# Moving GpSimd's tensor_tensor work to VectorE in a two-layer diffusion step, with more load buffers at the start and 370 GB/s for transfers in the list schedule

## The chip, the cores and the metric

The kernel runs on one core of one Trainium2 chip. The metric is the device time of one execution in microseconds (us), the median of several runs. Engines are named as in the profile: PE is TensorE (matmuls; PEld its weight loads), DVE is VectorE, ACT is ScalarE, POOL is GpSimd, SP is SyncE, which issues every DMA of this kernel.

## The reference

One inference step of a diffusion backbone, two layers deep, in float32. There are 512 latent tokens and 128 context tokens, handled together as five tiles of 128 tokens. Per layer:

```
mod = silu(cond) @ w_mod + b_mod                 # 6 vectors of 1024, one set for latents, one for context
h = rmsnorm(x) * (1 + sc1) + sh1
z = h @ w_in                                     # queries, keys, values of three mixers, and the gates
mix A: windowed attention with a sink; mix B: latent attention; mix C: full attention with rotary
m = sum over mixers of sigmoid(gate) * (o @ w_o) ;  x = x + g1 * rmsnorm(m @ w_out)
h = rmsnorm(x) * (1 + sc2) + sh2
x = x + g2 * rmsnorm(square(relu(h @ w_mlp1)) @ w_mlp2)      # 1024 -> 4096 -> 1024
```

The outputs are the two token sets and, for the context tokens, each layer's keys and values.

## The kernel before

**Arithmetic.** Nearly every matmul is done with float32 operands split in two: a high part (ACT, a copy to the reduced type) and a low part (DVE, source minus high part), and three products high*high, high*low, low*high (`mm3`). So each weight tile costs one ACT and one DVE instruction beside its matmuls. The split of a loaded weight unit is `wh`/`wl` in the profile.

**Stages of a layer.** First the modulated norm; then the projections and heads of mixer B (`b_proj`, `b_rope`, `b_heads`); then mixers A and C (`gqa_proj`, `gqa_qproj`, `gqa_group`), called the A/C stage below; then the gated merge (`merge`), the output projection (`wout`), the first MLP matrix (the up stage: `mlp1_first`, `sums`, `mlp1_pair`) and the second (the down stage: `mlp2_block`, `kblock`). The modulation vectors of later stages (`mod_gen`) and the gates (`gate_gen`) are side streams that are fed in between. In the first layer the A/C stage lies at about 300 to 550 us and the up stage at 780 to 970; in the second at 1450 to 1700 and 1940 to 2120.

**The up stage.** Output columns are taken in 14 pairs of 128-column tiles per layer. `mlp1_pair` forms a seven-product scheme: it loads a 128 x 2048 block `wq`, forms four sums `s1..s4` of its quarters (the profile's `s`, from lines with `tt = ...`), splits seven operands, and multiplies each by a split block of the activations or of the activation sums `t0..t3` that `sums` makes once per layer out of `hfull`.

**The modulation stream.** `mod_gen` multiplies each 128x512 piece of `w_mod` by a per-partition scalar and accumulates it, for two conditionings: `macc` 0 with one DVE instruction, `macc` 1 with a scaling on ACT and an addition on POOL.

**What POOL does.** Its tensor_tensor work is: the second `macc`, the four sums of each pair, the last addition of the rotary embedding (`ra`), the merge's addition (`m`), the residual addition of the first two token tiles (`xr`), the context's softmax normalisation (`pt<-pt,den`) and 128x1 or 128x4 powers (`rs`, `hrs`). It also does tensor_scalar work with one tensor input: the softmax normalisation of the latents (`pt<-pt,rc`) and the first norm's scaling (`xn`).

**The start.** `first_norm` loads the five token tiles `x` (three buffers) and eight 128 x 2048 blocks `mw` of `w_mod` (four buffers), multiplies the latter by the conditioning on PE (64 matmuls `lps<-mw,scT`), transposes the normed tokens on PE (`nps`) and modulates them.

**What sets the order.** The program is recorded, not issued: `Recorder.record` gives each operation a cost (`cost`), `one` simulates the engines with these costs and takes at each moment the ready operation of lowest rank, `latest` walks back from the end and gives every operation its latest start, which is the rank in the next of eight passes; PE keeps its program order as rank. The plan with the earliest end is emitted, so each engine's instruction order is fixed by it. In the plan a POOL tensor_tensor with over four elements per partition (`both`) runs 1.2 times as long, and a DVE operation without a PSUM operand that meets one is lengthened by up to 0.62 of the overlap. A DMA is planned on one shared network at 300 GB/s (line 470 in `one`), after 1.6 us and with 0.7 us behind it. SP takes its transfers in planned order. All instructions have line 528 in the profile, where the plan is emitted, so rows are told apart by tile names.

Of the kernel before, what the change touches and what calls it, by code (L numbers as in the profile page):

```python
# [11 lines left out]
F32 = mybir.dt.float32  # L12
F32R = mybir.dt.float32r
AF = mybir.ActivationFunctionType
# [3 lines left out]
P = 128  # L18
D = 1024
# [148 lines left out]
class Recorder:  # L168
# [192 lines left out]
    def latest(self, everything, end):  # L361

        for o in everything:
            o.late = end
        before, gave = {}, {}
        last = None
        for o in self.done:
            if o.eng == "tensor":
                before[o], last = last, o
        for p, t in self.given:  # L370
            gave.setdefault(t, []).append(p)
        for o in reversed(self.done):
            for p, data in o.preds.items():
                t = o.late
                if data:
                    t -= p.end - p.start
                    if o.eng is not None and p.eng != o.eng:
                        t -= self.LAT
                p.late = min(p.late, t)
            for p in gave.get(o, ()):  # L380
                p.late = min(p.late, o.late)
            p = before.get(o)
            if p is not None:
                p.late = min(p.late, o.late - p.busy)

    def one(self, everything, look):
# [49 lines left out]
        while True:  # L436
            best = None
            for e in engines:
                if now[e]:
                    t = free[e]  # L440
                elif later[e]:
                    t = max(free[e], later[e][0][0])
                else:
                    continue
                if best is None or t < best[0]:
                    best = (t, e)
            if best is None:
                break
            t, e = best
            ready, soon = now[e], later[e]  # L450
            while soon and soon[0][0] <= t:
                _, c, o = heapq.heappop(soon)
                heapq.heappush(ready, (o.rank, c, o))
            if look and soon and e in ("vector", "scalar", "gpsimd"):

                come = [r for r, c, u in heapq.nsmallest(6, soon) if r < t + ready[0][2].busy and u.rank < ready[0][0] - self.URGENT]
                if come:
                    fit = [q for q in ready if t + q[2].busy <= come[0] + 0.03]
                    if not fit:
                        free[e] = come[0]  # L460
                        continue
                    q = min(fit)
                    ready.remove(q)
                    heapq.heapify(ready)
                    heapq.heappush(ready, (-1e9, q[1], q[2]))
            o = heapq.heappop(ready)[2]
            o.start = t
            busy, wait = o.time
            if o.dma:
                net = max(net, t + 1.6) + wait / 300e3  # L470
                wait = net + 0.7 - t
            elif e == "vector" and o.sb and pool_end > t:
                more = 0.62 * min(pool_end - t, busy / 0.38)
                busy, wait = busy + more, wait + more
            elif o.both:
                busy, wait = 1.2 * busy, 1.2 * wait
                pool_end = t + busy
            elif e == "tensor":
                if t - free[e] > 2.6:
                    half = t + (6.8 if t - free[e] > 4 else 3.4)  # L480
                if t < half:
                    busy, wait = 2 * busy, wait + busy
            free[e] = t + busy
            o.busy, o.end = busy, t + wait
            order.append(o)
            self.done.append(o)
            release([o])
# [44 lines left out]
class Step:  # L532
# [182 lines left out]
    def mod_gen(self, mp, l, vecs, own=0):  # L715
# [3 lines left out]
        for v in vecs:  # L719
            for hf in range(2):  # L720
                c0 = v * D + hf * 512
                acc = [mp.tile([P, 512], F32, name=f"macc{s}", tag=f"macc{s}", bufs=1) for s in range(2)]
                for u in range(4):
# [6 lines left out]
                    for j in range(2):  # L730
                        k = 2 * u + j
                        s0, s1 = self.scT[:, 0, k:k + 1], self.scT[:, 1, k:k + 1]
                        if k == 0:
                            nc.vector.tensor_scalar(acc[0], rv[:, j, :], s0, None, ALU.mult)
                            nc.scalar.activation(acc[1], rv[:, j, :], AF.Copy, scale=s1)
                        else:
                            nc.vector.scalar_tensor_tensor(out=acc[0], in0=rv[:, j, :], scalar=s0, in1=acc[0],
                                                           op0=ALU.mult, op1=ALU.add)
                            nc.scalar.activation(rv[:, j, :], rv[:, j, :], AF.Copy, scale=s1)
                            nc.gpsimd.tensor_tensor(acc[1], acc[1], rv[:, j, :], ALU.add)  # L740
                    yield
                isg = v in (2, 5)
                if isg:
# [79 lines left out]
    def first_norm(self, pool, xin):  # L823

        nc, I = self.nc, self.I
        self.cond()
        xs = [pool.tile([P, D], F32, name="x0", tag="x0", bufs=3) for t in range(NT)]
        for t in range(NT):
            nc.sync.dma_start(xs[t], xin[t])
        hf = pool.tile([P, KC, T], F32, name="hf0")  # L830
# [12 lines left out]
        for n in range(2):  # L843
            if n == 1:
                self.first = self.proj_units(I["w_in"][0], 768 + 384, 288, 3)
            for v in (1, 0):
                ps = self.lin_ps()
                for kh in range(2):
                    raw = pool.tile([P, 4, 512], F32, name="mw", tag="mw", bufs=4)
                    nc.sync.dma_start(raw, self.wsrc(w, 4 * kh, 4, v * D + n * 512, 512))  # L850
                    for i in range(4):
                        k = 4 * kh + i
# [287 lines left out]
    def prompt_group(self, pool, qT, kT, kv, sink):  # L1140
# [22 lines left out]
            nc.scalar.activation(es, es, AF.Exp)  # L1163
            nc.vector.tensor_tensor(den, den, es, ALU.add)
        nc.vector.reciprocal(den, den)
        nc.gpsimd.tensor_tensor(p3, p3, den.unsqueeze(2).to_broadcast([P, 4, P]), ALU.mult)
        yield
        self.ppt = pt

# [27 lines left out]
    def kv_evac(self, pool, l, mixer, kT, V):  # L1197
# [3 lines left out]
        def evac(t, ps):  # L1201
# [6 lines left out]
            def turn():  # L1208
                if norm:
                    norm()  # L1210
                if t < 4:
                    cs = (self.cosA, self.sinA) if isA else (self.cosK, self.sinK)
                    res["k"] = self.rope(pool, k, 2, cs[0][:, t], cs[1][:, t], 16, nc.gpsimd)
                    self.put_v(V, t, v)
                else:
                    if not isA:
# [17 lines left out]
    def q_evac(self, pool, mixer, qT):  # L1234
# [3 lines left out]
        def evac(t, ps):  # L1238
# [5 lines left out]
            def turn():  # L1244
                if norm:
                    norm()
                if t < 4:
                    cs = (self.cosA, self.sinA) if isA else (self.cosQ, self.sinQ)
                    res["q"] = self.rope(pool, q, 4, cs[0][:, t], cs[1][:, t], 16, nc.gpsimd)
                elif isA:  # L1250
                    res["q"] = q
                else:
# [160 lines left out]
    def b_rope(self, keep, pool, l):  # L1413
# [5 lines left out]
        for t in range(NT):  # L1419
# [4 lines left out]
                         wl[:, k].rearrange("p h d -> p (h d)"), k == 0, k == 2)  # L1424
            pv = ps[:, :256].rearrange("p (h d) -> p h d", h=8)
            if t < 4:
                r = self.rope(pool, pv, 8, self.cosB[:, t], self.sinB[:, t], 8, nc.gpsimd)
                nc.scalar.activation(self.qr[:, t], r, AF.Copy)
            else:
                nc.scalar.activation(self.qr[:, t], pv, AF.Copy)  # L1430
# [161 lines left out]
    def merge(self, pool, l, mh, ml):  # L1592
# [12 lines left out]
        for n2 in range(4):  # L1605
# [5 lines left out]
            for i, b in enumerate((1, 0, 2)):  # L1611
                for e in range(2):
# [12 lines left out]
                        out=dst.rearrange("p (a n) -> p a n", a=2), in0=th.rearrange("p (a n) -> p a n", a=2), scalar=1.0,  # L1625
                        in1=ps[:, :, :NH], op0=ALU.add, op1=ALU.mult)
                    if i:
                        nc.gpsimd.tensor_tensor(m, m, th, ALU.add)
                    yield
            for e in range(2):  # L1630
                n, m = 2 * n2 + e, ms[e]
# [51 lines left out]
    def post(self, pool, l, w, src, f, t, xsrc, out):  # L1683
# [7 lines left out]
        r = self.rstd(src, D, jk, 2 if last or src is not f else 1)  # L1691
        for c in (slice(0, 512), slice(512, D)) if last else (slice(0, D),):
            nc.vector.scalar_tensor_tensor(out=f[:, c], in0=src[:, c], scalar=r, in1=self.gg[:, s, c], op0=ALU.mult, op1=ALU.mult)
            (nc.vector if t >= 2 else nc.gpsimd).tensor_tensor(x[:, c], x[:, c], f[:, c], ALU.add)
            nc.sync.dma_start(out[:, c], x[:, c])
        return x

# [67 lines left out]
    def mlp1_pair(self, pool, l, n, t, halfs, keep=None):  # L1765
# [7 lines left out]
        sa = pool.tile([P, 2, 4, P], F32, name="s12", tag="s12", bufs=2)  # L1773
        sb = pool.tile([P, 2, 4, P], F32, name="s34", tag="s34", bufs=2)
        s1, s2, s3, s4 = sa[:, 0], sa[:, 1], sb[:, 0], sb[:, 1]
        tt = nc.gpsimd.tensor_tensor
        tt(s1, a21, a22, ALU.add)
        tt(s2, s1, a11, ALU.subtract)
        tt(s3, a11, a21, ALU.subtract)
# [376 lines left out]
```

## Time and profile before

| quantity | value |
| --- | --- |
| median of 3 runs | 2357.48 us (2355.71 to 2359.46) |
| profiled execution | 2356.36 us, span 2354.6 us, mean granted clock 0.995 |
| PE busy | 2286.6 us (97%) |
| DVE busy | 1700.6 us (72%) |
| ACT busy | 1289.2 us (55%) |
| POOL busy | 763.2 us (32%) |
| DMA | 317 MB, mean 135 GB/s |

The span is the profiled execution from its first to its last instruction; what lies around it is 1.8 us. Busy is the time in which an engine had an instruction running. Ends of matmuls are modelled and overlap with the next one, so a busy PE can still have lost some time; where that matters, matmuls are counted per stretch instead.

### The profile page before, as it was taken

What the parts mean: (1) busy time and instruction counts of PE and PEld (TensorE: products, weight loads), DVE (VectorE), ACT (ScalarE), POOL (GpSimd) and SP (SyncE); (2) the same over time, 40 slices, a digit from 0 to 9 for tenths busy, and PEclk for the clock granted to TensorE, in tenths of its full rate; (3) what the DMA queues carried; (4) which work ended last, traced back from release to release, by engine and by line L of the source; (5) the groups of instructions that cost most, each with busy time, mean ns of one, the idle gap of its engine ahead of it and who ended that gap; (6) DMA issues with size and microseconds to landing.
All of it is one profiled execution on the core that took longest, in us unless ns stands there. A gap on an engine that the chain in (4) does not pass through costs nothing. (4 is left out here: it accounts for less than half of the span.)

```text
span 2354.6 us, 39546 instructions
## 1 busy us (share of the span) xinstructions
PE 2286.6 (97%) x14303; PEld 2089.6 (89%) x14303; DVE 1700.6 (72%) x3351; ACT 1289.2 (55%) x3000; POOL 763.2 (32%) x671
## 2 busy tenths in 40 slices
PE   8999999999999999999999999999999999999998
PEld 3988999989998999888889889899999889998886
DVE  3778488897675998867477866998846669884444
ACT  4577466676435565744265765767743356664222
POOL 1322044562132475223033212455412315650001
PEclk9999999999999999999999999999999999999999
DMA  7431244343663454664244222434346544446332
GB/s 252 112 91 50 86 121 129 104 107 96 218 208 113 149 170 146 224 209 150 80 134 113 65 82 75 127 105 125 109 152 187 177 135 150 165 139 215 117 120 81
DMA packets 252451, 317.10 MB, mean 135 GB/s; under 512 B 37328, under 2 KB 169696, under 8 KB 251744
## 3 DMA queue, kind: packets, MB, share of 16 engines
q1 hardware_dynamic: 252256, 314.58, 42.9%
q8 instruction: 113, 1.85, 0.3%
q14 instruction: 82, 0.67, 0.1%
HBM read 251.84 MB, written 57.44 MB: 131 GB/s over the span
## 5 line engine op out<-in xcount | busy, mean ns | idle before, releaser
L528 DVE TENSOR_TENSOR wl<-wr,wh 128x256 fp32r<-128x256 f32 (+5 forms) x772 | 370.5, 527 | 145.0 <-ACT wh L528 143.6
L528 ACT ACTIVATE wh<-wr 128x256 fp32r<-128x256 f32 (+5 forms) x772 | 276.2, 421 | 257.5 <-PE lps L528 140.0
L528 POOL TENSOR_SCALAR pt<-pt,rc 128x640 f32<-128x640 f32 (+1 forms) x192 | 167.4, 879 | 315.3 <-DVE rc L528 261.2
L528 PE MATMUL lps<-wh,ah 128*128 128x512 f32 x640 | 252.8, 395 | 0.0
L528 PE MATMUL lps<-wh,al 128*128 128x512 f32 x640 | 252.4, 394 | 0.0
L528 PE MATMUL lps<-wl,ah 128*128 128x512 f32 x640 | 251.9, 394 | 0.0
L528 POOL TENSOR_TENSOR rs<-ss,mhalf 128x1 f32<-128x1 f32 x60 | 37.1, 619 | 497.5 <-DVE ss L528 496.6
L528 DVE TENSOR_TENSOR pl<-tps,ph 128x512 fp32r<-128x512 f32 (+2 forms) x240 | 147.8, 631 | 30.3 <-ACT ph L528 27.6
L528 ACT ACTIVATE pt<-sps,nm 128x640 f32<-128x640 f32 (+2 forms) x192 | 141.7, 741 | 50.9 <-DVE nm L528 48.6
L528 PE MATMUL sps<-h2h,wl 128*128 128x320 f32 (+2 forms) x464 | 145.0, 313 | 9.8 <-DVE wl L528 9.8
L528 ACT ACTIVATE ph<-tps 128x512 fp32r<-128x512 f32 (+2 forms) x240 | 130.4, 555 | 33.0 <-PE tps L528 29.9
L528 PE MATMUL sps<-h2h,wh 128*128 128x320 f32 (+2 forms) x464 | 145.9, 314 | 0.0
L528 PE MATMUL tps<-ident,pt 128*128 128x128 f32 x896 | 140.5, 275 | 5.2 <-POOL pt L528 1.9
L528 PEld LDWEIGHTS lps<-wl,ah 128*128 128x128 f32 x640 | 120.1, 188 | 28.5 <-issue 0.2
L528 PEld LDWEIGHTS lps<-wh,ah 128*128 128x128 f32 x640 | 120.1, 188 | 28.0 <-issue 0.5
L528 PE MATMUL sps<-h2l,wh 128*128 128x320 f32 (+2 forms) x464 | 144.6, 312 | 0.0
L528 PEld LDWEIGHTS lps<-wh,al 128*128 128x128 f32 x640 | 120.1, 188 | 27.5
L528 POOL TENSOR_TENSOR macc<-macc,wr 128x512 f32<-128x512 f32 x84 | 118.3, 1409 | 57.2 <-ACT wr L528 44.4
L528 POOL TENSOR_TENSOR s<-wq 128x512 f32<-128x512 f32 x56 | 89.8, 1604 | 142.4 <-DMA wq<-in_w_mlp 116.9
L528 POOL TENSOR_TENSOR macc<-macc,mr 128x512 f32<-128x512 f32 x56 | 87.7, 1566 | 140.5 <-ACT mr L528 92.9
L528 DVE TENSOR_TENSOR wl<-s,wh 128x512 fp32r<-128x512 f32 x112 | 123.3, 1114 | 3.4 <-ACT wh L528 2.2
L528 PE MATMUL gps<-hh,wh 128*128 128x320 f32 x384 | 120.1, 313 | 2.2 <-ACT th L528 1.7
(335 smaller groups left out, 7371.4 us busy)
## 6 DMA issues: line engine op xcount, KB each, us to landing
wr<-in_w_in SPq DMA_DIRECT2D x72, 512.0 KB, 3.8
wr<-in_w_mlp SPq DMA_DIRECT2D x72, 512.0 KB, 4.0
wq<-in_w_mlp SPq DMA_DIRECT2D x56, 512.0 KB, 4.1
wr<-in_w_mod SPq DMA_DIRECT2D x48, 512.0 KB, 3.8
ar<-a SPq DMA_DIRECT2D x56, 320.0 KB, 4.5
mr<-in_w_mod SPq DMA_DIRECT2D x32, 512.0 KB, 4.6
th<-th SPq DMA_DIRECT2D x96, 160.0 KB, 1.9
tg<-th SPq DMA_DIRECT2D x48, 320.0 KB, 3.1
```

What stands on the lines that cost most here:

```text
L528: getattr(getattr(self.nc, o.eng), o.name)(*args, **kw)
```

## The change

All POOL tensor_tensor instructions over whole tiles become DVE instructions. In `mod_gen` the pair "scale on ACT, add on POOL" becomes one DVE scalar_tensor_tensor. POOL keeps the powers and the tensor_scalar work. The first norm gets five buffers for `x` and eight for `mw`. The plan counts transfers with 370 GB/s, and in the backward pass a transfer counts its own 2.3 us plus bytes/370e3 in place of the time between its planned issue and landing.

```
             for p, data in o.preds.items():
                 t = o.late
                 if data:
-                    t -= p.end - p.start
+                    t -= 2.3 + p.wait / 370e3 if p.dma else p.end - p.start
...
-                net = max(net, t + 1.6) + wait / 300e3
+                net = max(net, t + 1.6) + wait / 370e3
...   mod_gen
-                            nc.scalar.activation(rv[:, j, :], rv[:, j, :], AF.Copy, scale=s1)
-                            nc.gpsimd.tensor_tensor(acc[1], acc[1], rv[:, j, :], ALU.add)
+                            nc.vector.scalar_tensor_tensor(out=acc[1], in0=rv[:, j, :], scalar=s1, in1=acc[1],
+                                                           op0=ALU.mult, op1=ALU.add)
...   first_norm
-        xs = [pool.tile([P, D], F32, name="x0", tag="x0", bufs=3) for t in range(NT)]
+        xs = [pool.tile([P, D], F32, name="x0", tag="x0", bufs=5) for t in range(NT)]
-                    raw = pool.tile([P, 4, 512], F32, name="mw", tag="mw", bufs=4)
+                    raw = pool.tile([P, 4, 512], F32, name="mw", tag="mw", bufs=8)
...   prompt_group
-        nc.gpsimd.tensor_tensor(p3, p3, den.unsqueeze(2).to_broadcast([P, 4, P]), ALU.mult)
+        nc.vector.tensor_tensor(p3, p3, den.unsqueeze(2).to_broadcast([P, 4, P]), ALU.mult)
...   kv_evac, q_evac, b_rope: rope(..., nc.gpsimd) becomes rope(..., nc.vector)
...   merge
-                        nc.gpsimd.tensor_tensor(m, m, th, ALU.add)
+                        nc.vector.tensor_tensor(m, m, th, ALU.add)
...   post
-            (nc.vector if t >= 2 else nc.gpsimd).tensor_tensor(x[:, c], x[:, c], f[:, c], ALU.add)
+            nc.vector.tensor_tensor(x[:, c], x[:, c], f[:, c], ALU.add)
...   mlp1_pair
-        tt = nc.gpsimd.tensor_tensor
+        tt = nc.vector.tensor_tensor
```

## Rows read from the trace of the kernel before

**Rows 1.** The page's engines: busy us (share of the span), instructions.
```profile
PE 2286.6 (97%) x14303; PEld 2089.6 (89%) x14303; DVE 1700.6 (72%) x3351; ACT 1289.2 (55%) x3000; POOL 763.2 (32%) x671
```

**Rows 2.** Waits of PE, whole span: us in total, times, longest us.
```profile
PE sps L528 <- DVE wl L528: 9.8, 2, 5.1
...
PE nps L528 <- POOL xn L528: 2.8, 1, 2.8
```

**Rows 3.** Stretches where the up stages begin: busy us (instructions), PEclk, DMA share, GB/s.
```profile
785.00:790.00 5.00, 1.11 (x5) 1.11 (x6) 5.00 (x4) 2.81 (x7) 4.92 (x4) 0.91 0.00 0
...
1940.00:1945.00 5.00, 0.33 (x1) 0.33 (x2) 5.00 (x4) 2.03 (x5) 4.92 (x4) 0.78 0.00 0
1945.00:1950.00 5.00, 5.00 (x21) 5.00 (x21) 5.00 (x4) 3.41 (x9) 4.14 (x3) 0.54 0.16 52
```

**Rows 4.** Timeline of DVE, second up stage: start us, us, what.
```profile
1932.78 0.82 DVE L528 TENSOR_TENSOR t1l<-hfull,t1h 128x640 fp32r<-128x640 f32 x1
...
1935.72 3.75 DVE L528 TENSOR_TENSOR t0l<-hfull,t0h 128x640 fp32r<-128x640 f32 x2
1939.39 1.75 DVE L528 TENSOR_TENSOR wl<-wq,wh 128x512 fp32r<-128x512 f32 x1
...
1950.35 0.68 DVE L528 TENSOR_TENSOR wl<-wq,wh 128x512 fp32r<-128x512 f32 x1
```

**Rows 5.** Timeline of POOL in the same stretch.
```profile
1935.59 1.38 POOL L528 TENSOR_TENSOR s<-wq 128x512 f32<-128x512 f32 x1 [17.02 <-DMA wq<-in_w_mlp]
```

**Rows 6.** Timeline of PE in the same stretch.
```profile
1944.67 0.64 PE L528 MATMUL sps<-h2h,wl 128*128 128x320 f32 x1 [5.12 <-DVE wl L528]
```

**Rows 7.** Groups of instructions, whole span: count | busy us, mean ns.
```profile
L528 POOL TENSOR_TENSOR macc<-macc,wr 128x512 f32<-128x512 f32 x84 | 118.3, 1409 | 57.2 <-ACT wr L528 44.4 <-issue 6.9 <-DVE rc L528 2.2
L528 POOL TENSOR_TENSOR s<-wq 128x512 f32<-128x512 f32 x56 | 89.8, 1604 | 142.4 <-DMA wq<-in_w_mlp 116.9 <-DVE u L528 8.8 <-DVE wl L528 8.3
L528 POOL TENSOR_TENSOR m<-m,tg 128x640 f32<-128x640 f32 x32 | 55.1, 1723 | 186.5 <-DMA tg<-th 87.6 <-DVE tg L528 79.3 <-issue 10.9
L528 DVE TENSOR_TENSOR wl<-s,wh 128x512 fp32r<-128x512 f32 x112 | 123.3, 1114 | 3.4 <-ACT wh L528 2.2
```

**Rows 8.** Stretches inside the first A/C stage and the first up stage.
```profile
300.00:550.00 250.00, 240.79 (x1751) 228.97 (x1751) 224.46 (x506) 163.86 (x418) 123.37 (x117) 1.00 0.41 119
800.00:950.00 150.00, 150.00 (x1017) 149.04 (x1016) 133.85 (x190) 92.50 (x158) 94.94 (x59) 1.00 0.50 165
```

**Rows 9.** Groups of instructions between 300 and 550 us.
```profile
L528 DVE TENSOR_TENSOR wl<-wr,wh 128x256 fp32r<-128x256 f32 x80 | 43.3, 585 | 0.9 <-ACT wh L528 0.8
L528 DVE SCALAR_TENSOR_TENSOR macc<-wr,scT,macc 128x512 f32<-128x512 f32 x35 | 30.8, 881 | 0.4
...
L528 POOL TENSOR_TENSOR ra<-ra,rb 128x256 f32<-128x256 f32 x12 | 11.1, 928 | 16.7 <-DVE rb L528 11.1 <-DVE hss L528 4.2 <-DVE ra L528 1.4
```

**Rows 10.** Timeline of DVE where POOL has nothing to do.
```profile
1912.39 1.41 DVE L528 SCALAR_TENSOR_TENSOR f<-fps,rs,gg 128x512 f32<-128x512 f32 x2 [0.66 <-POOL rs L528]
...
1914.92 1.42 DVE L528 TENSOR_TENSOR wl<-wr,wh 128x256 fp32r<-128x256 f32 x4
```

**Rows 11.** Timelines of DVE and of POOL in the A/C stage, one moment.
```profile
481.46 1.52 DVE L528 TENSOR_TENSOR pz<-pz,hrs 128x256 f32<-128x256 f32 x1
...
481.26 1.44 POOL L528 TENSOR_TENSOR macc<-macc,wr 128x512 f32<-128x512 f32 x1
```

**Rows 12.** Stretches of the start.
```profile
28.00:32.00 4.00, 1.17 (x8) 1.10 (x8) 0.89 (x5) 1.95 (x5) 1.77 (x2) 0.91 1.06 389
32.00:36.00 4.00, 4.00 (x16) 1.22 (x15) 0.96 (x5) 1.29 (x3) 0.00 (x0) 0.66 1.06 393
```

**Rows 13.** Timelines of SP and PE at the start.
```profile
20.20 0.38 SPq L528 DMA_DIRECT2D x<-in_x_prompt  x1
...
30.90 1.62 PE L528 MATMUL nps<-ident,xn 128*128 128x128 f32 x8 [2.83 <-POOL xn L528]
```

**Rows 14.** DMA issues on the page: count, KB each, median us to landing.
```profile
wr<-in_w_in SPq DMA_DIRECT2D x72, 512.0 KB, 3.8
```

More of the change, by code (lines that the diff above doesn't have):

```diff
@@ L1212, in turn @@
                     cs = (self.cosA, self.sinA) if isA else (self.cosK, self.sinK)
-                    res["k"] = self.rope(pool, k, 2, cs[0][:, t], cs[1][:, t], 16, nc.gpsimd)
+                    res["k"] = self.rope(pool, k, 2, cs[0][:, t], cs[1][:, t], 16, nc.vector)
                     self.put_v(V, t, v)
@@ L1248, in turn @@
                     cs = (self.cosA, self.sinA) if isA else (self.cosQ, self.sinQ)
-                    res["q"] = self.rope(pool, q, 4, cs[0][:, t], cs[1][:, t], 16, nc.gpsimd)
+                    res["q"] = self.rope(pool, q, 4, cs[0][:, t], cs[1][:, t], 16, nc.vector)
                 elif isA:
@@ L1426, in b_rope @@
             if t < 4:
-                r = self.rope(pool, pv, 8, self.cosB[:, t], self.sinB[:, t], 8, nc.gpsimd)
+                r = self.rope(pool, pv, 8, self.cosB[:, t], self.sinB[:, t], 8, nc.vector)
                 nc.scalar.activation(self.qr[:, t], r, AF.Copy)
```

## The prediction

> **What bounds the kernel now.** The page's engine line comes first: PE is busy 97% of the span, DVE 72%, POOL 32% [rows 1]. So a change that touches no matmul can win only what PE loses. A busy PE hides part of that, since ends of matmuls are modelled; the matmuls of a stretch, counted, show it. Inside an up stage PE issues 1017 matmuls in 150 us, one per 0.1475 us, without a gap [rows 8]; there nothing can be won. The list of what PE waited for comes second. Its largest line is a wait for `wl`, 9.8 us in two pieces [rows 2]: both lie where the up stages begin, one per layer. The third view is a table of stretches there: PE has 5 matmuls in one 5 us stretch of the first layer, and 1 and then 21 in two such stretches of the second, where 34 would fit, and the granted clock of these falls to 0.78 and 0.54 [rows 3], so in part to the lower of the two levels. The fourth view is the start, with a wait of 2.8 us for the last token tile [rows 2], again with a lower clock behind it, 0.66 [rows 12]. In the first A/C stage PE is idle for 250 - 240.8 = 9.2 us, in small pieces, beside a DVE that is busy 224.5 of 250 us [rows 8].
>
> **The beginning of the up stage.** The stall of PE is a chain on DVE. Two `t0l` take 3.75 us, a split `wl` 1.75 us; the neighbouring `t1l` of the same shape took 0.82 us and a later split of the same shape 0.68 us [rows 4]. What differs is POOL: from 1935.59 us on it forms the sums `s` [rows 5]. So each of these DVE instructions loses about 1 us. The stall ends with a `wl` at 1944.67 us after 5.12 us [rows 6], and the matmuls behind it come 0.24 us apart (21 in 5 us [rows 3]) instead of 0.1475, until the clock is back.
>
> After the change POOL does nothing here, and DVE does the four sums itself. I lay DVE's work for the first pair out from 1935.72 us, when PE still has matmuls up to 1939.5 us (1944.67 less 5.12 [rows 6]). The distance between two DVE instructions of 128x512 is about 0.62 us (0.68 less the overlap that the start times show). First split and sums s1 and s2 (three) end at 1937.6; two more splits at 1938.8; two `t0l` at 0.75 at 1940.3. PE needs the first split at once, and the third operand two products later (each product is 12 matmuls, 1.8 us), at 1943. The whole pair costs DVE 7 splits and 4 sums of 0.62, two `t0l`, two `hfull` and two `t3l` of 0.75 and seven additions of about 0.42, so 14.3 us against 7 products of 1.77 = 12.4 us on PE, which starts 3.7 us later than DVE. So PE has no long wait left. What goes is 9.8 us of waiting, and from the slow matmuls (21 in the 5 us stretch where 34 fit, 13 times 0.1475 = 1.9 us, and about 1 us in the first layer) 2.9 us: 12.7 us. I take -12, for some small waits left. Bounds: -13 if all goes; 0 if DVE orders the sums so badly that the same chain stands.
>
> **Inside the up stage.** Here the cover is what matters: PE is full, DVE busy 133.9 of 150 us, POOL 94.9 [rows 8]. The 59 POOL instructions go to DVE at 0.62 to 0.7 us, 37 us more. In return the splits get shorter: the 112 splits of sums took 1.114 us on average [rows 7] and take 0.68 where POOL is idle [rows 4]; an instruction in 150 us out of 12 pairs with 7 splits each gives 84 times about 0.42, 35 us back. So DVE stays at about 136 of 150, PE stays full, and the term is 0. Its bounds stand under the rivals.
>
> **The A/C stage.** Per layer 35 of the `macc` additions (their DVE partners are in [rows 9]) go to DVE as scalar_tensor_tensor of 0.705 us (two in 1.41 [rows 10]): 24.7 us; with twelve rotary additions [rows 9] at the 0.355 us of a 128x256 instruction on a quiet DVE [rows 10], 4.3 us, and a few smaller ones, about 31 us. Back come, from the two largest groups alone, 80 splits at 43.3/80 = 0.54 against 1.42/4 = 0.355 us: 14.9 us, and 35 `macc` at 0.88 against 0.705: 6.1 us [rows 9, 10]; smaller groups with two SBUF inputs give more. One is seen frozen: a 128x256 multiplication takes 1.52 us, until POOL's `macc` that began 0.2 us earlier is through [rows 11]. So DVE goes from 224.5 to between 227 and 234 of 250 us; ACT loses the 35 scalings and POOL 35 times 1.41 [rows 7] and 11.1 [rows 9], 60 us, so POOL's normalisations no longer stand behind a `macc`. PE's 9.2 us of idle time (the second layer is taken as alike) come partly from such freezes, partly from the load itself. I take -3 for both layers, near zero because DVE's load does not fall. Bounds: -18 (all idle time of both) to +10.
>
> **The start.** The fifth tile `x_prompt` is issued only at 20.20 us, when a third buffer comes free, and PE waits for it at 28 to 30.9 us [rows 13]. With five buffers that wait goes: 2.8 us, and about 1.3 us for the stretch at 0.66 of the clock [rows 12] (a third of 4 us). The transfers are no shorter: at 389 to 393 GB/s they are already at the rate of the whole start [rows 12], and the bytes stay. Taken: -4. Bounds: -6 (the transposes and modulation matmuls pack without any gap) to +3 (all five tiles, 2.6 MB, are taken ahead of the first `mw`: 2.6 MB less the two tiles that lead now is 1.6 MB, 4 us at 390 GB/s, on PE's first matmuls).
>
> **The merge, the residual additions and the plan's rates.** The 32 additions `m` took POOL 1.72 us each [rows 7] and become 0.75 us on DVE; the matmuls of the next tiles lie over them, and without that cover only the last one of a layer's merge would show, 1.5 us over both layers: 0. The first two tiles' residual addition, 1.2 us as two pieces of 128x512, has three later tiles' matmuls over it: 0. A 512 KB transfer is planned at 2.3 + 524288/370e3 = 3.7 us; it landed after 3.8 [rows 14]; with 300 it was 4.05. The plan is no worse fed, but SP's order and the due times of whatever frees a buffer move everywhere: 0, bounds -5 to +8 (two of the loading stretches in each layer late by half a landing of 3.8 us).
>
> **Sum.** -12 - 4 - 3 = -19 on the profiled execution's 2356.36 us (a span of 2354.6 and 1.8 around it), 2337.4; the median of the runs shown lies 1.1 us higher: 2338 us.
>
> **Rivals.**
> *VectorE becomes the bound of the up stages.* It gets 37 us in 150, and would stand at 171 of 150 us if nothing came back [rows 8]. Two up stages are 2.2 such stretches. With a quarter of the expected 35 us back, it lacks 133.9 + 37 - 9 - 150 = 12 us per stretch, 26 us in all, and -19 turns into +7: 2364 us. It decides where less than 12 us of the 35 come back per stretch. For it: DVE is at 89% there now. Against it: split times of 0.68 and 1.75 us, apart only by POOL's activity [rows 4, 5]. A sentence of the Trainium skill bears on this chance: SBUF — State Buffer, section Who interferes with whom, says that a VectorE instruction with two SBUF inputs and a GpSimd instruction that reads SBUF exclude each other for a whole instruction rather than share. By that rule the whole loss comes back, and the frozen instruction [rows 11] agrees; by a partial sharing, as the plan has it, some two thirds would.
>
> *Half of the up-stage stall stays.* The first `wq` block lands only at 1935.5 us [rows 5]; if DVE takes four sums before the first split, or the block lands later under the new order, PE waits some 2.5 us per layer and the clock falls with it. Then 12 shrinks to 6: 2344.
>
> *The new plan costs elsewhere what it wins.* One list, eight passes, other costs: orders change in every stage. With +8 from late transfers 2346; with the start at +3 as well and the A/C stage at +5, the sum is about -3: 2354, no change.
>
> *The change does not do what it says at the start.* The plan may issue the last `x` as late as now: then 4 us less, 2342; it is inside the forecast's own range.
>
> **How the numbers follow.** The forecast with its own range of 2329 to 2343 gets 0.62, half a stall 0.12, late transfers 0.08, all faster by over 0.2% (4.7 us, about what a measurement of this kernel can tell from no change). No change gets 0.09, slower (VectorE the bound, or more of the A/C stage's +10) 0.09. So faster 0.82, same 0.09, slower 0.09. The range that leaves 2 in 10 out runs from 2325, where the A/C stages win most of their idle time, to 2355.
>
> **What would show each step.** In the changed profile: POOL's busy time falls by more than half; DVE stays within 1700 to 1760 us; ACT falls by 60 to 100. The split `wl<-s` has a mean near 0.68 us. PE's wait for `wl` where the up stages begin is under 2 us and the granted clock there stays at 1.00. The wait for `xn` at the start is gone, and the first `sps` matmuls begin some 4 us earlier. The forecast is wrong if PE shows gaps inside an up stage, if PE's idle time in the A/C stages grows by over 5 us each, or if DVE is busy for over 1800 us.

## The result and the profile after

The changed kernel takes 2330.95 us, the median of 4 runs (2327.95 to 2336.26), against 2357.09 us of before: a ratio of 0.9891, 95% interval [0.9867, 0.9914]. The forecast was 2338 us, faster; the medians lie 26.1 us apart where it had 19. The profiled execution took 2327.95 us with a span of 2326.2, so 28.4 us less than before.

The engines line of the page answers to [rows 1]:

```profile
PE 2277.6 (98%) x14303; PEld 2086.7 (90%) x14303; DVE 1705.0 (73%) x3707; ACT 1204.0 (52%) x2860; POOL 260.8 (11%) x315
```

DVE has 356 instructions more and is busy only 4.4 us longer; POOL loses 502 us and ACT 85. Why DVE's time stays is read in its groups (count | busy us, mean ns | idle before), the first answering to [rows 7], the third to [rows 9]:

```profile
L528 DVE TENSOR_TENSOR wl<-s,wh 128x512 fp32r<-128x512 f32 x112 | 74.6, 685 | 5.4 <-ACT wh L528 4.9
L528 DVE TENSOR_TENSOR m<-m,tg 128x640 f32<-128x640 f32 x32 | 26.3, 822 | 0.5
L528 DVE SCALAR_TENSOR_TENSOR macc<-wr,scT,macc 128x512 f32<-128x512 f32 x168 | 126.4, 786 | 6.0 <-DMA wr<-in_w_mod 5.7
```

The split `wl<-s` falls from 1114 to 685 ns. PE's waits over the whole span, against [rows 2]: the line for `wl` is gone, what was second and third stands ahead.

```profile
PE rowps L528 <- DMA wr<-in_c_ctx: 6.2, 1, 6.2
PE ops L528 <- DVE pl L528: 5.8, 10, 1.8
PE sps L528 <- DVE qd L528: 4.3, 6, 0.8
PE tps L528 <- POOL pt L528: 2.9, 6, 0.7
PE ops L528 <- DVE oraw L528: 2.6, 5, 1.5
```

Where the up stages begin ([rows 3] of before; columns as there), PE has 37 to 45 matmuls in each 5 us, at a granted clock of 1.00, that is the level of 2.4 GHz:

```profile
770.00:775.00 5.00, 5.00 (x45) 5.00 (x43) 5.00 (x9) 3.98 (x10) 0.00 (x0) 1.00 0.88 287
775.00:780.00 5.00, 5.00 (x37) 5.00 (x36) 5.00 (x8) 4.03 (x9) 0.00 (x0) 1.00 0.09 31
...
1915.00:1920.00 5.00, 5.00 (x43) 5.00 (x42) 5.00 (x9) 3.98 (x10) 0.00 (x0) 1.00 0.52 168
```

DVE's timeline of that stretch answers to [rows 4]: sums and splits alternate 0.6 us apart, and `t0l` takes 0.82 us, where two took 3.75.

```profile
772.23 0.68 DVE L528 TENSOR_TENSOR wl<-wq,wh 128x512 fp32r<-128x512 f32 x1
772.83 0.68 DVE L528 TENSOR_TENSOR s<-wq 128x512 f32<-128x512 f32 x1
773.43 0.68 DVE L528 TENSOR_TENSOR wl<-wq,wh 128x512 fp32r<-128x512 f32 x1
...
775.24 0.82 DVE L528 TENSOR_TENSOR t0l<-hfull,t0h 128x640 fp32r<-128x640 f32 x1
```

The stretches inside the A/C and the up stage, against [rows 8], and those of the start, against [rows 12]:

```profile
300.00:550.00 250.00, 244.19 (x1787) 233.82 (x1786) 229.24 (x570) 145.38 (x385) 66.03 (x67) 1.00 0.42 121
800.00:950.00 150.00, 150.00 (x1016) 149.00 (x1016) 138.46 (x256) 87.72 (x155) 0.00 (x0) 1.00 0.47 154
```

```profile
28.00:32.00 4.00, 4.00 (x11) 0.74 (x9) 0.00 (x0) 0.59 (x1) 0.00 (x0) 1.00 1.05 386
32.00:36.00 4.00, 4.00 (x13) 1.00 (x13) 2.51 (x6) 2.90 (x5) 0.00 (x0) 1.00 1.07 386
```

**Stage by stage.** PE's matmuls are the same 14303 in every kernel here, so a stage's length can be taken from the first matmul of one kind to the first of another. In this table "start" is the time of the first `lps<-wh,qlh`; "A/C" runs from the first `sps<-kT,qT` to the first `sps<-oh` of a layer (in the kernel before from 291.1 to 602.0 and from 1446.8 to 1758.7 us, so it is longer than the 250 us of [rows 8]); "up" from the first `fps<-wh,mh` (output projection) to the first `lps<-wh,ah`, with the up stage in it. The granted clock of the A/C stretch stands behind it, to two places. Lengths are read to 0.1 us. Ratios are each against the kernel before in runs on the same chip; its median was 2359.52 us beside the four kernels "before + ...", 2361.16 beside the four "undone" ones from the macc to the buffers, 2357.39 beside the last four, so times in us compare only within such a group.

| kernel | start | A/C 1 (clock) | A/C 2 (clock) | up 1, 2 | ratio [95%] |
| --- | --- | --- | --- | --- | --- |
| before | 97.0 | 310.9 (1.00) | 311.9 (1.00) | 268.1, 269.1 | 1 |
| after | 93.7 | 306.0 (1.00) | 309.0 (1.00) | 261.7, 261.3 | 0.9891 [0.9867, 0.9914] |
| before + sums | 96.5 | 310.7 (1.00) | 310.8 (1.00) | 261.7, 261.5 | 0.9925 [0.9912, 0.9938] |
| before + macc | 97.5 | 309.3 (0.99) | 314.5 (0.98) | 269.1, 265.7 | 0.9993 [0.9983, 1.0003] |
| before + buffers | 99.6 | 309.2 (1.00) | 314.7 (0.99) | 265.7, 266.9 | 0.9996 [0.9988, 1.0005] |
| before + rates | 102.4 | 311.3 (1.00) | 311.3 (0.99) | 265.0, 265.3 | 1.0006 [0.9996, 1.0016] |
| after, macc undone | 93.9 | 317.2 (0.98) | 313.1 (0.99) | 261.6, 261.3 | 0.9922 [0.9910, 0.9935] |
| after, small moves undone | 94.1 | 307.7 (0.99) | 311.3 (0.99) | 261.7, 261.5 | 0.9887 [0.9874, 0.9901] |
| after, rates undone | 99.8 | 307.7 (0.99) | 311.6 (0.99) | 261.6, 261.4 | 0.9910 [0.9897, 0.9924] |
| after, buffers undone | 101.4 | 309.3 (0.98) | 309.5 (0.99) | 261.6, 261.4 | 0.9920 [0.9908, 0.9933] |
| after + POOL additions | 94.0 | 307.0 (0.99) | 308.1 (1.00) | 275.6, 277.0 | 1.0039 [1.0025, 1.0052] |
| after + POOL memsets | 94.2 | 306.3 (1.00) | 309.2 (0.99) | 261.6, 261.3 | 0.9895 [0.9882, 0.9909] |
| after, rate alone undone | 94.1 | 306.9 (0.99) | 307.9 (1.00) | 261.6, 261.4 | 0.9871 [0.9856, 0.9886] |
| after, `pt` on ACT | 94.2 | 301.4 (1.00) | 305.2 (0.99) | 261.6, 261.3 | 0.9895 [0.9882, 0.9909] |

So of the 28.4 us, 14.2 come in the two up stretches (6.4 and 7.8), 7.8 in the A/C stages (4.9 and 2.9), 3.3 at the start; between the layers (first `lps<-wh,ah` to the second layer's `lps<-wh,qlh`, 290.3 to 288.2) 2.1; small ones make the rest.

### The profile page after: what moved, and what is told of

Its sections match the earlier page's. It is cut to its first block, busy times and chain, and to the rows that moved or that the text cites. A ratio compares the mean times of both kernels' runs of the same rounds, so it can differ in the third digit from the quotient of the medians.

```text
span 2326.2 us, 39127 instructions
## 1 busy us (share of the span) xinstructions
PE 2277.6 (98%) x14303; PEld 2086.7 (90%) x14303; DVE 1705.0 (73%) x3707; ACT 1204.0 (52%) x2860; POOL 260.8 (11%) x315
## 5 line engine op out<-in xcount | busy, mean ns | idle before, releaser
L528 DVE TENSOR_TENSOR wl<-wr,wh 128x256 fp32r<-128x256 f32 (+5 forms) x772 | 303.4, 441 | 147.9 <-ACT wh L528 143.0
L528 POOL TENSOR_SCALAR pt<-pt,rc 128x640 f32<-128x640 f32 (+1 forms) x192 | 174.1, 915 | 629.4 <-DVE rc L528 523.2
L528 DVE TENSOR_TENSOR pl<-tps,ph 128x512 fp32r<-128x512 f32 (+2 forms) x240 | 147.9, 630 | 31.1 <-ACT ph L528 28.4
L528 DVE SCALAR_TENSOR_TENSOR macc<-wr,scT,macc 128x512 f32<-128x512 f32 x168 | 126.4, 786 | 6.0 <-DMA wr<-in_w_mod 5.7
L528 PE MATMUL gps<-h2h,wh 128*128 128x320 f32 x384 | 119.7, 312 | 0.2 <-DVE pl L528 0.2
L528 PEld LDWEIGHTS tps<-ident,pt 128*128 128x128 f32 x896 | 106.7, 141 | 14.5 <-POOL pt L528 5.5
L528 PE MATMUL sps<-ol,wh 128*128 128x320 f32 x384 | 118.6, 309 | 0.5 <-DVE ol L528 0.5
```

Of the source, the lines that this page charges most:

```text
L528: getattr(getattr(self.nc, o.eng), o.name)(*args, **kw)
```

## The experiments

**The sums alone**, on the kernel before:

```
-        tt = nc.gpsimd.tensor_tensor
+        tt = nc.vector.tensor_tensor
```

> The kernel before, with only the four sums of each up-stage pair formed on VectorE. My theory: POOL's reading additions slow VectorE while PE stands, so this one line takes the two waits for wl (9.8 us) and the slow matmuls behind them, and VectorE's splits of sums fall from 1.11 to about 0.7 us: 12 to 14 us faster, about 2343 us against 2357. Rival 1, the list schedule's new rates and order do it: then this line alone gives under 4 us (above 2353). Rival 2, VectorE becomes the bound of the up stage: 2364 or more, and PE matmuls missing inside 800 to 950 us.

Measured: 2341.16 us (2339.95 to 2343.36), ratio 0.9925, so 18 us faster than before on the same chip (2359.52) and 16.1 us less span: more than the 12 to 14 that I expected. Both up stretches have the length that they have in the whole change, to 0.2 us, and PE's wait for `wl` at `sps` is down to 0.3 us. This line of the change is over half of it; the new rates are not needed for it, and VectorE's load is no bound. The table shows one thing more: with the sums still on POOL, the plans of "before + rates" and "before + buffers" shorten the two up stretches together by 6.9 and 4.7 us, and PE's waits for `wl` there fall from 9.8 us to 4.9 and 5.6. So how long the frozen chain holds PE up depends on the order of the plan as well, and the kernel before had a poor one; the sums on VectorE are what takes the wait away whole.

**The macc alone**, on the kernel before:

```
-                            nc.scalar.activation(rv[:, j, :], rv[:, j, :], AF.Copy, scale=s1)
-                            nc.gpsimd.tensor_tensor(acc[1], acc[1], rv[:, j, :], ALU.add)
+                            nc.vector.scalar_tensor_tensor(out=acc[1], in0=rv[:, j, :], scalar=s1, in1=acc[1],
+                                                           op0=ALU.mult, op1=ALU.add)
```

> The kernel before, with only the second macc as one VectorE scalar_tensor_tensor in place of a scaling on ACT and an addition on POOL. The A/C stages of the changed kernel gained 7.8 us where I had put 3. My theory: the macc additions on POOL were what froze VectorE there, so this alone gives 4 to 8 us (2349 to 2353), nearly all of it between the first kT and the merge of both layers, and nothing at the up stage's beginning (PE's wait for wl stays near 9.8). Rival: the A/C gain came with the rotary additions or the new rates; then within 2 us of before, 2355 to 2357, since VectorE's load there doesn't fall.

Measured: 2358.07 us, ratio 0.9993: by the time, my theory failed. The profile shows what hid it. These are the two A/C stages of this kernel, and inside the first one two stretches where the granted clock fell, so partly to 1.2 GHz:

```profile
293.00:602.30 309.30, 301.63 (x2156) 287.97 (x2154) 263.17 (x628) 181.40 (x471) 92.55 (x99) 0.99 0.39 113
...
1449.20:1763.70 314.50, 305.19 (x2155) 289.47 (x2154) 260.24 (x620) 183.37 (x472) 90.36 (x99) 0.98 0.39 113
```

```profile
525.00:535.00 10.00, 9.79 (x60) 9.01 (x60) 9.38 (x23) 6.54 (x16) 4.12 (x4) 0.83 0.52 141
495.00:505.00 10.00, 9.20 (x55) 8.98 (x56) 8.82 (x25) 5.02 (x12) 1.53 (x2) 0.83 0.37 118
```

To three places the clock's records give 0.989 and 0.984, so some 3.4 and 5.1 us of full speed are lost. Without that the stages would take some 306 and 309 us, as in the whole change. The runs say the same when those of one mean clock are compared: at 0.994 this kernel took 2354.99 us (one run) where before took 2358.88 (mean of 13), at 0.993 2353.90 (one) against 2361.41 (9), at 0.992 2357.68 (2) against 2364.59 (2). These are few runs, and a thousandth of the clock is some 2 us, so the figures are rough; but at a given clock the macc wins 4 to 8 us, as the theory had it. Only, this kernel runs at a mean clock of 0.990 to 0.994 where before has 0.992 to 0.995, and that takes the gain away again. Why its clock is lower the runs don't show. The reverse tests it once more.

**The buffers alone and the rates alone**, on the kernel before:

```
-        xs = [pool.tile([P, D], F32, name="x0", tag="x0", bufs=3) for t in range(NT)]
+        xs = [pool.tile([P, D], F32, name="x0", tag="x0", bufs=5) for t in range(NT)]
-                    raw = pool.tile([P, 4, 512], F32, name="mw", tag="mw", bufs=4)
+                    raw = pool.tile([P, 4, 512], F32, name="mw", tag="mw", bufs=8)
```

> The kernel before, with only the buffers of the first norm raised: five for x, eight for mw. My theory: the wait for the fifth token tile (2.8 us) and the slow clock behind it are all that the start gained (3.3 us), so 3 to 4 us faster, 2353 to 2354. Rival: the start's gain needs the plan's new rates (its order of the first transfers), then under 1 us here.

```
-                    t -= p.end - p.start
+                    t -= 2.3 + p.wait / 370e3 if p.dma else p.end - p.start
-                net = max(net, t + 1.6) + wait / 300e3
+                net = max(net, t + 1.6) + wait / 370e3
```

> The kernel before, with only the plan's transfer rate at 370 GB/s and its new backward formula; every instruction stays on its engine. My theory: no more than 2 us to either side (2355 to 2359), since PE waits for DMA under 10 us in all. Rival: the new plan is what gains at the change of layers (2.1 us) and in the A/C stages (7.8): then 5 to 10 us faster, 2347 to 2352.

Measured: 2358.30 (ratio 0.9996) and 2361.56 us (1.0006). Neither moves the time, and each makes the start worse, by 2.6 and 5.4 us: the theory for the buffers failed. SP's timelines say why. First the buffers alone, then the rates alone, then the whole change (start us, us, what):

```profile
3.60 0.36 SPq L528 DMA_DIRECT2D x<-in_x_prompt  x1
4.00 2.34 SPq L528 DMA_DIRECT2D mw<-in_w_mod  x4
6.39 4.87 SPq L528 DMA_DIRECT2D x<-in_x_sample  x4
```

```profile
7.37 2.11 SPq L528 DMA_DIRECT2D mw<-in_w_mod  x3
16.36 1.19 SPq L528 DMA_DIRECT2D x<-in_x_sample  x1
...
21.88 1.11 SPq L528 DMA_DIRECT2D x<-in_x_prompt  x1
```

```profile
6.51 0.97 SPq L528 DMA_DIRECT2D x<-in_x_sample  x2
7.53 0.67 SPq L528 DMA_DIRECT2D mw<-in_w_mod  x1
8.25 0.50 SPq L528 DMA_DIRECT2D x<-in_x_prompt  x1
8.80 13.41 SPq L528 DMA_DIRECT2D mw<-in_w_mod  x6
```

With more buffers and the old costs, four 1 MB blocks `mw` go ahead of the four latent tiles, and the first transposes start at 22.97 us (7.75 after the whole change):

```profile
22.97 1.10 PE L528 MATMUL nps<-ident,xn 128*128 128x128 f32 x8
```

With the new costs and three buffers `x_prompt` leaves at 21.88 us (20.20 before [rows 13]), and PE runs at the lower level behind the wait, the clock standing at 0.50:

```profile
32.00:36.00 4.00, 1.66 (x8) 1.57 (x8) 0.67 (x5) 0.51 (x1) 2.19 (x2) 0.50 1.05 396
```

Only both together give the order that wins 3.3 us.

**One part of the change undone at a time.** The macc (its diff above, reversed):

> The changed kernel with the second macc back as ACT scaling and POOL addition. Taken alone the macc gave nothing in the time (2358), but its profile has 43 us of TensorE's lower clock level against 25 before, and PE busy in the first A/C stage rose from 240.8 to 243.8 of 250 us. Theory: in the whole change the macc is what gives the A/C stages their 7.8 us, so this loses 4 to 8 us: 2335 to 2339 against 2331, with kT to merge back near 311 us in each layer. Rival: the A/C gain comes from the rotary and the other additions; then within 2 us, 2329 to 2333.

The small moves:

```
-   rope(..., nc.vector) in kv_evac, q_evac, b_rope; nc.vector.tensor_tensor for m, for pt<-pt,den and for x of tiles 0 and 1
+   the same with nc.gpsimd
```

> The changed kernel with the smaller moves back on POOL: the rotary additions, the context's softmax normalisation, the merge's addition m and the residual addition of two tiles; the sums and the macc stay on VectorE. I predicted 0 for merge and residual and a few us for the rotary additions. Theory (macc makes the A/C gain): 0 to 4 us slower, 2331 to 2335. Rival (the rotary additions make it): 5 to 9 us slower, 2336 to 2340. If DVE's load were what counts in the A/C stages, it would be faster by some us.

The rates and the buffers (their diffs above, reversed):

> The changed kernel with the plan's transfer costs of before (300 GB/s and the old backward formula). Alone the rates lost 5 us at the start and the buffers alone lost 3, while together with the rest the start won 3. Theory: the start needs both, since with 300 GB/s the plan takes all token tiles ahead of the first mw; so this is 4 to 8 us slower, 2335 to 2339, nearly all by the first lps<-wh,qlh. Rival, the rates are worth nothing: within 2 us, 2329 to 2333.

> The changed kernel with three buffers for x and four for mw again. Theory: the wait for the fifth token tile and the lower clock behind it come back at the start, 3 to 6 us slower, 2334 to 2337, nothing elsewhere by itself. Rival: with the rates in force the start's order is what counts and the buffers nothing: within 2 us, 2329 to 2333.

Measured: macc 2342.23, small moves 2334.18, rates 2339.86, buffers 2341.36 us. Without the macc's move the ratio is 0.9922, 0.3% worse than the whole change (the intervals touch at 0.991), with both A/C stages longer than in the whole change (317.2 and 313.1 against 306.0 and 309.0):

```profile
287.50:604.70 317.20, 305.45 (x2154) 289.53 (x2153) 266.52 (x611) 201.32 (x505) 124.59 (x114) 0.98 0.37 110
```

To three places the clock is 0.984 and 0.995; less its share (5.1 and 1.7 us) that is 312 and 311, the lengths of before.

The small moves undone: the ratio is the same (0.9887), A/C less the clock's share (1.7 us in each) 306 and 310, against 306.0 and 309.0 in the whole change. They are worth nothing that can be measured. These two kernels ran on the same chip, and at one mean clock of 0.997 the one without the macc took 2342.23 us (one run), the one without the small moves 2333.77 (mean of three); at 0.995 2344.21 against 2337.36 (one each). So the theory holds: the macc makes the A/C gain, the rotary additions don't.

The rates undone: the start takes 99.8 us, with the first transposes at 23.14 us, late as in the buffers-only kernel. The theory holds in size, but not in the order that it gave: four `mw` blocks go ahead of the latent tiles, not the tiles ahead of `mw`. The ratio's interval [0.9897, 0.9924] overlaps with the change's; against the kernel without the small moves, on the same chip at the same mean clocks, it is 5 us slower (2338.82 against 2333.77 at 0.997, 2342.69 against 2337.36 at 0.995).

The buffers undone: PE's wait for `xn` is back (4.5 us in three pieces), the start takes 101.4, 7.7 us more than in the change and worse than before it, a little more than the 3 to 6 expected; the clock in the A/C stages is lower too, and nothing is gained elsewhere.

**VectorE as the bound: POOL's additions put back as dead work**, on the changed kernel, behind a pair's last addition `u`:

```
+        dm = pool.tile([P, 4, P], F32, name="dm", tag="dm", bufs=1)
+        for _ in range(4):
+            nc.gpsimd.tensor_tensor(dm, s3, s4, ALU.add)
```

> The changed kernel with work added: four POOL additions of 128x512 per up-stage pair, SBUF to SBUF, on the sums s3 and s4, into a tile that nothing reads. Nothing is added to VectorE or TensorE. This tests my rival that VectorE becomes the bound of the up stage, by taking back what the change was to give back. Theory: a VectorE instruction that meets such an addition is frozen. In the profile before, 112 sums on POOL cost VectorE's splits about 75 us; as many additions cost about that again. VectorE has 11.5 of 150 us free in the up stage, 12 pairs cost 30 us, so the up stages get longer by some 18 us per 150: 2345 to 2375, PE shows gaps inside 800 to 950, and wl<-s is near 1.1 us again. Rival (POOL's reads cost nothing; the gain was one of order): 2329 to 2333, wl<-s at 0.69.

and as the control:

```
+        for _ in range(8):
+            nc.gpsimd.memset(s3, 0.0)
```

> The control to the added additions: at the same place eight POOL memsets of 128x512 per pair, which write SBUF but read nothing. Theory (it is POOL's reading beside VectorE's two SBUF inputs): no change, 2329 to 2335, and wl<-s stays near 0.69 us. Rival (any busy POOL slows VectorE): as with the additions, in proportion to POOL's busy time.

Measured: 2368.57 us with the additions (ratio 1.0039, slower than the kernel before), 2333.03 with the memsets (0.9895, as the change). The same stretch of the up stage with additions, then with memsets:

```profile
800.00:950.00 150.00, 140.65 (x922) 136.55 (x921) 149.69 (x214) 76.22 (x131) 70.69 (x44) 0.99 0.42 137
```

```profile
800.00:950.00 150.00, 150.00 (x1017) 149.04 (x1016) 131.09 (x241) 84.19 (x148) 50.65 (x96) 1.00 0.46 151
```

With additions DVE is full (149.69 of 150) with fewer instructions done (214 against 256), and PE loses 94 of 1016 matmuls. The groups of the first kernel:

```profile
L528 DVE TENSOR_TENSOR wl<-s,wh 128x512 fp32r<-128x512 f32 x112 | 101.7, 912 | 1.6 <-ACT wh L528 1.6
L528 DVE TENSOR_TENSOR wl<-wq,wh 128x512 fp32r<-128x512 f32 x84 | 91.7, 1093 | 0.0
...
L528 POOL TENSOR_TENSOR dm<-s 128x512 f32<-128x512 f32 x112 | 186.8, 1668 | 236.3 <-DVE s L528 229.8
```

and of the second:

```profile
L528 DVE TENSOR_TENSOR wl<-s,wh 128x512 fp32r<-128x512 f32 x112 | 74.5, 685 | 6.8 <-ACT wh L528 6.6
...
L528 POOL MEMSET s<- 128x512 f32 x224 | 118.2, 528 | 257.3 <-DVE wl L528 246.0
```

224 memsets, 118 us of a busy POOL, leave the split at 685 ns. It is POOL's reading instructions, not a busy POOL. How they do it is seen in one group of four additions of the first kernel, POOL's timeline and then DVE's:

```profile
861.72 6.72 POOL L528 TENSOR_TENSOR dm<-s 128x512 f32<-128x512 f32 x4 [6.29 <-DVE s L528]
```

```profile
862.50 1.38 DVE L528 TENSOR_TENSOR wl<-wq,wh 128x512 fp32r<-128x512 f32 x1
863.81 1.77 DVE L528 TENSOR_TENSOR wl<-s,wh 128x512 fp32r<-128x512 f32 x1
865.51 0.48 DVE L528 TENSOR_TENSOR r<-sps,u 128x320 f32<-128x320 f32 x1
```

The first two additions end at 863.33 and 865.03 us, the two splits at 863.88 and 865.58, 0.55 us behind each; `r`, which has one of its inputs in PSUM, takes no longer than elsewhere.

DVE's busy time rises by 83 us (1705.0 to 1788.4) for 187 us of additions; the up stretches get 14 and 16 us longer. Of the 196 splits of the two groups (from the timeline) 126 take under 0.70 us, 68 take 1.26 to 1.79 and two lie between. The lengths alone don't tell a stop from a shared rate: in the kernel before the 107 slow splits of these groups are spread from 0.77 to 1.8 us. The ends do. Each of these 107, and each of the 70 here, ends 0.545 to 0.556 us behind the end of a POOL instruction that reads, whether it takes 0.77 us in all or 1.8; alone it takes 0.68. A shared rate would give no such fixed distance: the split stands until POOL is through and then does its work. And the 74 DVE additions `r` and `u` that overlap a `dm` by over 0.15 us, with one input in PSUM (`sps`), take 477 ns on average, against 476 to 478 away from it. The Trainium skill (SBUF — State Buffer, section Who interferes with whom) calls the contention of a VectorE instruction that has two SBUF inputs with a GpSimd instruction that reads SBUF an exclusive lock, which this agrees with; the section also excepts GpSimd instructions that only write SBUF, and the memsets agree.

**The formula or the rate**, on the changed kernel:

```
-                net = max(net, t + 1.6) + wait / 370e3
+                net = max(net, t + 1.6) + wait / 300e3
```

> The changed kernel with the forward simulation at 300 GB/s again, but the new backward formula kept (a transfer counts 2.3 us plus its bytes, not its planned wait in the queue). Undoing both cost 9 us: there four blocks of mw are issued ahead of the first x tiles. Theory: the formula, not the rate, sets that order, since with the old one a transfer that is planned behind others looks longer and is called earlier: 2329 to 2335, x tiles first. Rival: the rate does it: 2336 to 2341, with the first transposes at 23 us.

Measured: 2328.06 us, ratio 0.9871 [0.9856, 0.9886], with the good order of the start. Against the rates undone (0.9910 [0.9897, 0.9924]) the intervals are apart: what wins is the backward formula, which no longer counts a transfer's planned wait in the queue. The 370 GB/s are worth nothing that shows; the intervals of this kernel and of the change overlap.

**A try for more: the last reading work off POOL**, on the changed kernel:

```
-        nc.gpsimd.tensor_scalar(pt[:, :w], pt[:, :w], rc, 1.0, ALU.mult, ALU.mult)
+        nc.scalar.activation(pt[:, :w], pt[:, :w], AF.Copy, scale=rc)
```

> The changed kernel with POOL's last large reading work moved too: the normalisation of the softmax tiles (192 tensor_scalar, 174 us) becomes an ACT copy with a scale. A try for a faster kernel. For it: some VectorE instructions beside pt take 1 us longer, and PE waits 2.9 us for pt. Against it: ACT gets about 0.75 us each, some 60 us more in each A/C stage, where it is busy 145 of 250 us, and ph stands behind it. Theory: 2 to 6 us faster, 2325 to 2329. Rival: ACT's queue delays ph and the evacuations: 2333 to 2345.

Measured: 2333.62 us, ratio 0.9895: no gain in all, but it wins and loses in different stages. The first A/C stage gets 4.6 us shorter than in the whole change, the second 3.8; mixer B's heads get 7.4 and 5.1 us longer. Mixer B's stretch of the first layer (first `sps<-kTb` to first `sps<-kT,qT`), in the change and then here:

```profile
121.00:287.90 166.90, 161.66 (x1149) 150.93 (x1150) 119.13 (x284) 106.79 (x266) 30.48 (x40) 1.00 0.26 73
```

```profile
121.30:295.60 174.30, 164.92 (x1149) 152.70 (x1150) 118.97 (x284) 129.57 (x306) 0.00 (x0) 0.99 0.25 70
```

```profile
PE sps L528 <- ACT pt L528: 6.8, 10, 1.4
```

The last line is this kernel's largest wait of PE. The rival is what came true in mixer B. `pt` on ACT in the A/C stages and on POOL in mixer B should win some 8 us by these lengths, an estimate; that version was not run.

## Why the prediction was right, and where not

In all the terms gave -19, and the profiled execution became 28.4 us shorter: 2.2 us more than forecast at the beginning of the up stages, 4.8 more in the A/C stages, 0.7 less at the start, and 3.1 between the layers and in small pieces that no term had.

*The beginning of the up stages (-12; measured 14.2).* Right in place and cause. The sums alone remove the wait and the slow matmuls; DVE laid out as I had it (0.6 us between neighbours, `t0l` at 0.74). Of the wait of 9.8 and the 2.9 us of slow matmuls all is back. Most of the other 1.5 us lies in the slow matmuls, which the sum had too small: in PE's timeline of before 13 intervals behind the first wait take 3.51 us and 18 behind the second 4.95, so 31 intervals lose 3.9 us against 0.1475 each, 1.6 in the first layer (where the sum had about 1) and 2.3 in the second (1.9).

*Inside the up stage (0; measured 0).* 1016 matmuls in 150 us as before, DVE at 138.5 where I had 136. The rival was real and near (at 12 pairs per 150 us the 28 pairs are 2.3 such stretches, not 2.2, which makes its price 2 us higher): 11.5 us of DVE's 150 were left, and putting the reads back beside DVE cost 35 us of time (1.0039 against 0.9895 with the memsets, on the same chip). What decided is that the frozen time comes back.

*The A/C stages (-3 for both layers; measured 7.8).* The mis-sized term. DVE's load between 300 and 550 us stayed within what I gave (229.2 of 250, with 1787 matmuls done instead of 1751). From the two groups that I priced less came back than I said: the 128x256 split fell to 35.6/84 = 0.42 us, not 0.355, a `macc` to 53.4/70 = 0.76, not 0.705; smaller groups made up for it, and over the whole stages DVE's busy time went from 265.2 to 264.8 us in the first layer and from 256.9 to 263.1 in the second. I took a small gain because the load doesn't fall. But PE's idle time there is made mostly of waits for one late DVE instruction: 8.6 of 9.4 us in the first stage, 6.0 of 9.8 in the second. The largest of the first stage, before and then after:

```profile
PE ops L528 <- DVE oraw L528: 3.8, 4, 1.8
PE kps L528 <- DVE kst L528: 1.4, 3, 0.7
PE ops L528 <- DVE pl L528: 1.2, 4, 0.7
```

```profile
PE ops L528 <- DVE pl L528: 2.2, 3, 1.8
PE ops L528 <- DVE oraw L528: 2.0, 3, 1.5
```

The longest one of before stands behind a `macc` chain, as timelines of DVE, POOL and PE show:

```profile
511.72 4.68 DVE L528 TENSOR_TENSOR wl<-wr,wh 128x256 fp32r<-128x256 f32 x4
```

```profile
511.75 4.37 POOL L528 TENSOR_TENSOR macc<-macc,wr 128x512 f32<-128x512 f32 x3
```

```profile
517.28 0.47 PE L528 MATMUL ops<-ph,V 128*128 128x512 f32 x1 [1.81 <-DVE oraw L528]
```

Four splits take 4.68 us where four take 1.42 on a quiet DVE [rows 10]; the `oraw` that PE waits for comes next on DVE. With the `macc` gone from POOL these waits fell from 9.4 to 6.2 and from 9.8 to 6.3 us, 6.7 of the 7.8 us, at a load that did not fall. Not every wait was of this kind: of those that are left one is as long (1.8 us for `pl`), and the `pt` on ACT cut them further, to 2.7 and 3.7. The term should have been priced by those waits.

*The start (-4; measured 3.3).* The sum was near by luck, the steps were not right. The wait for `xn` fell from 2.8 to 0.9 us and did not go. "The first `sps` matmuls begin some 4 us earlier" is wrong: they begin at 45.23 us against 44.97; but by then all matmuls with `mw` are done, which before went on among them (the last began at 50.29, now at 44.71), so what follows comes earlier. And I gave the gain to the buffers. Alone they cost 2.6 us, by the way that I had as the bound of +3, only with the other order: the `mw` blocks went ahead of the tiles. The plan's formula, which I put at 0, is what the buffers need.

*The plan's rates (0).* Alone 0 in the time, but no part of it is 0. In the profiled execution, the slowest of its twelve (2364.87 us), the start is 5.4 us longer, mixer B's first projections (first `lps<-wh,qlh` to first `sps<-kTb`) 4.7 and the time behind the last up stretch 4.9, while the up stretches are 6.9 us shorter. So 0 was a sum of several things, inside the bounds given.

*Merge, residual, small moves (0; measured 0).* Right. The 2.1 us between the layers I had not foreseen; no single part's run gives or takes them clearly, so their cause is open.

## What to carry to other kernels

Price a POOL instruction that reads SBUF by what it freezes on VectorE as well as by its own time: here 187 us of them cost a nearly full VectorE 83 us, 118 us of memsets nothing, and VectorE instructions with one input in PSUM lost nothing. When VectorE's load stays the same but its instructions stop being late, stages gain whose waits are for single instructions. Edits that share a scheduler are not additive: three of the four parts that were run alone gave nothing in the time, and buffers without a transfer cost that ranks them rightly made the start worse.

## What the runs showed of the hardware that was not expected

The scatter of the runs goes with TensorE's granted clock: the changed kernel's four runs took 2327.95, 2328.11, 2333.80 and 2336.26 us at mean clocks of 0.998, 0.998, 0.996 and 0.994; 0.004 of 2330 us is 9 us, about the distance seen. Which kernel gets a lower clock in its A/C stages doesn't follow from the length of its waits alone: in the first one before has 1.00 with 9.4 us of waits of PE, the macc-only kernel 0.99 with 7.4. What makes the difference is open; it decides whether a gain like the macc's shows in the time.

POOL's tensor_scalar on `pt` does less harm than its tensor_tensor: of the 128x256 splits of the changed kernel, the 44 that overlap one on 128x640 by over 0.15 us have a median of 417 ns, as the 633 that meet no POOL instruction, but a mean of 567, so only some are frozen. In the kernel before the 49 such splits that overlap a 128x512 tensor_tensor have a mean of 1007. Where a `pt` does freeze one, it ends about 0.27 us behind POOL's end, as behind a `macc` (0.28); what spares the others is open.
